# Four dense products of a hybrid encoder layer computed as seven block products of eight

## The chip, the cores and the metric

The kernel runs on one core of one Trainium2 chip. The metric is the device time of one execution in microseconds (us), the median of several runs. The profile is one further execution, recorded by the hardware profiler. PE is TensorE's matmul queue and PEld its weight loads, DVE is VectorE, ACT is ScalarE, POOL is GpSimd, SP the queue that issues the DMAs, SPq its issues.

## The reference, cut to what matters

512 positions and 16 meta positions of width 1024 pass one layer. Nothing but the products named here is changed:

```python
    y_conf = c @ w_conf_out                     # 1024 x 1024
    y_dn = o.reshape(b, l, HV) @ w_dn_out       # 1024 x 1024
    g_conf, g_dn = jnp.split(sigmoid(gate_logits + b_gate), 2, axis=-1)
    h = h + (g_conf * y_conf + g_dn * y_dn) @ w_out          # 1024 x 1024
    u2 = rmsnorm(h, norm_ffn_w)
    up = causal_dwconv(u2 @ w_up, ffn_dw_w, ffn_dw_b)        # 1024 x 5632, three taps
    f_gate, f_val = jnp.split(up, 2, axis=-1)
    return h + (jax.nn.silu(f_gate) * f_val) @ w_down
```

Before them stand one combined input projection, a causal convolution of 31 taps with a layer norm (it gives `c`), and a gated delta rule of 8 heads (it gives `o`). A final RMSNorm follows.

## The kernel before

Features lie on the 128 partitions and positions along the row, so an activation of width 1024 is eight tiles of 516 or 528 columns. Every dense product keeps float32 accuracy from operands split in two: `split` makes a rounded part `hi` (ScalarE) and the remainder `lo` (VectorE), and `gemm` sums `hi*hi`, `hi*lo` and `lo*hi` in one PSUM accumulation. For 128 output features that is 3 parts x 8 blocks of the depth x 2 halves of the positions, 48 matmuls of 258 or 260 columns, each with its own weight load. `weights` brings the 128 x 1024 weights of such a tile by a DMA on SP into `wr` (3 buffers), rounds them to `wh` on ScalarE and takes the remainder `wl` on VectorE (2 buffers each). The accumulators `p2` are two PSUM tiles of two banks each.

The order is: input norm and keys (`keys`), convolution gates (`glu`), the masked decays (`decays`, the only sizeable POOL work), Gram matrices (`grams`), `inverses` and `grow` (triangular inverses in 32-blocks), then the `heads` with gates `ga` and `z` between them. The 31 taps (`ca`) fill VectorE up to the end of the heads. Then come the delta-rule output projection (`gated`, tile `y`, operands `oh`, `ol`), the layer norm of the convolution and its output projection (`y` again, operands `ch`, `cl`), `w_out` (tile `wo`, operands `mh`, `ml`), the second norm and the feed-forward: `up` makes 44 output tiles, each scaled by the norm's `r` as it leaves PSUM (the norm is not needed before the product), and three taps make `uy` from it. Two `uy` give `fh` and `fl`, and `w_down` (tile `dn`) ends the layer.

Nothing runs in the order in which it is written. `Plan` records every instruction, `order` simulates five in-order engines with modelled costs (`price`), buffers (`SLOTS`) and priorities (`BIAS` and the named offsets), and `emit` issues the resulting fixed order through one helper line. So all instructions of the trace have the line of that helper, and they are told apart by tiles. What is fixed at build time is the order on each engine: where an instruction waits on the chip, all behind it on its engine wait too.

Of the kernel before, what the change touches and what calls it, by code (L numbers as in the profile page):

```python
# [19 lines left out]
P = 128  # L20
# [16 lines left out]
ROW = T + PAD  # L37

# [82 lines left out]
class Op:  # L121
    _fields = ("eng", "fn", "a", "k", "prio", "deps", "succ", "late", "wait", "cost", "ready", "end", "tiles", "lat", "table", "mode", "act", "tail", "alone")
# [21 lines left out]
TURN = {(False, True): 92, (True, False): 105, (True, True): 190}  # L144
# [6 lines left out]
STAY = 750  # L151
SWITCH = 600

BIAS = {'iv': -1500, 'd0': 100, 'v4': 40, 'v2': 100, 'z1': -570, 't11': -280, 't7': 350, 'k0': -70, 'ln': 250, 's7': -320, 'z0': -700, 'o2': 100, 'o5': 1600, 'd5': -650, 'g3': 150, 'd1': 2160, 'k2': -30, 'q7': -1720, 'k5': -30, 's4': -830, 'w3': -3100, 't2': -670, 'c5': -130, 't8': -40, 'o4': -350, 'q6': 350, 'g4': -350, 't4': -350, 'o1': 250, 'q4': -60, 't9': -750, 'z2': -600, 'o0': -600, 'g0': 30, 'q3': 500, 'q5': 100, 'c6': -30, 's1': -130, 't15': -100, 't1': -730, 's3': -470, 'y0': 250, 't12': -150, 'o6': 700, 'o3': -500, 'k4': -100, 'w2': 250, 't5': -150, 'v0': 30, 'g6': -120, 'z3': 250, 'g5': -190, 'q2': -70, 'y7': -30, 's5': -70, 'v6': -100, 'g1': -250, 'g7': 250, 'm4': 100, 'q0': -250, 'c7': -130, 'd3': -1750, 'o7': 100, 'm6': 30, 'm1': 30, 's6': -100, 'd2': -100, 'y6': 70, 'g2': -600, 'k6': -30, 'z4': -500, 't6': 100, 't3': 250}
LNP = 74
IVP = 1295
UP = 519
WP = 30
# [23 lines left out]

AFTER = 24
# [3 lines left out]
PARTS = (slice(1, 3), slice(0, 1))  # L187

# [9 lines left out]
class Plan:  # L198
# [9 lines left out]
    @contextmanager  # L208
    def at(self, by, late=True):
        if isinstance(by, str):  # L210
            by, late = BIAS.get(by, 0), False
        was = self.late
        self.prio, self.late = self.prio + by, was or late and by > 0
        yield
        self.prio, self.late = self.prio - by, was

    def add(self, eng, fn, a, k):
# [28 lines left out]
        if eng == "PE" and fn == "matmul":  # L246

            up = lambda n: 32 if n <= 32 else 64 if n <= 64 else P
            o.mode = (up(args[1].shape[0]), up(writes[0].shape[0]))
            o.mode = None if o.mode == (P, P) else o.mode  # L250
        o.cost, o.lat = self.price(eng, fn, a, k, writes[0])
        o.alone = self.price(eng, fn, a, k, writes[0], True)[0] if o.mode else o.cost
# [11 lines left out]
    def price(self, eng, fn, a, k, out, alone=False):  # L264
        n = out.n
        if eng == "PE":
            lhs, rhs = (k["lhsT"], k["rhs"]) if fn == "matmul" else (a[1], a[2])
            n = rhs.n
            if fn == "transpose":
                return 110, 0  # L270

            if out.ap.offset // out.tl.row and not alone:
                return 22, 0
# [3 lines left out]
            if lhs.shape[0] == 64:  # L277
                return 115, 0
# [13 lines left out]
    def order(self):  # L292
# [16 lines left out]
        table, dma, low, done = None, 0.0, 0, bytearray(len(ops))  # L309
        win, act, cold = 0, 0.0, True  # L310
        mode = None
# [14 lines left out]
        def look(e, t):  # L326

            q, nxt, best = ready[e], later[e][0][0] if later[e] else None, None
            for p, i in q:
# [26 lines left out]
                if e == "PE" and mode and o.mode != mode:  # L356
                    p += STAY
                elif o.table and table not in o.table:
                    p += SWITCH
# [4 lines left out]
        while len(out) < len(ops):  # L364
# [26 lines left out]
            if e == "PE":  # L391

                while t >= (win + 1) * WIN:
                    if act < LOW * WIN:
                        cold = True
                    elif act > HIGH * WIN:
                        cold = False
                    win, act = win + 1, 0.0
                if o.mode != mode:
                    c = o.alone + TURN[bool(mode), bool(o.mode)]  # L400
                if cold:
                    c *= 2
                act += o.act * (2 if cold else 1)
                mode = o.mode
            free[e] = t + c
            o.end = free[e]
            if e == "SP":
                dma = max(dma, t + 950) + o.lat
                o.end = dma + o.tail
            out.append(i)  # L410
# [10 lines left out]
            drain = 110 if o.mode else 0  # L421
            for j in o.succ:
                s = ops[j]
                s.ready = max(s.ready, o.end + LAT[e][s.eng] + (drain if s.eng != e else 0))
# [25 lines left out]
def record(A, out):  # L450
# [52 lines left out]
    def gemm(acc, ws, ah, al, ranges, k0=0, kn=None, first=True, last=True):  # L503
# [6 lines left out]
        for i, (k, w, a) in enumerate(runs):  # L510
            for b, (c0, c1, *at) in enumerate(ranges):
                p0 = at[0] if at else 0
                PE.matmul(acc[:, b, p0:p0 + c1 - c0], lhsT=w[:, k * P:(k + 1) * P], rhs=a[k0 + k][:, c0:c1],
                          start=first and i == 0, stop=last and i == len(runs) - 1)

# [263 lines left out]
    def decays(h):  # L779
# [5 lines left out]
                        compare_op=ALU.is_ge, fill=-1e30)  # L785
        for n in range(NC):
            S.activation(out=ev[:, n], in_=ev[:, n], func=AF.Exp, bias=ngc[:, n, h:h + 1])
# [46 lines left out]

    ivt = {}
# [136 lines left out]
    oh, ol = [], []  # L972
# [3 lines left out]
    def heads(h):  # L976
# [8 lines left out]
        with plan.at(f"s{h}"):  # L985
# [39 lines left out]
            for n in range(NC):  # L1025
# [18 lines left out]
                if n < NC - 1:  # L1044
                    s = s1

# [22 lines left out]
    def outs(h):  # L1069
# [5 lines left out]
        with plan.at(f"o{h}"):  # L1075
# [5 lines left out]
            a, b = split(z[:, :TW], TW, "o")  # L1081
            oh.append(a)
            ol.append(b)
# [38 lines left out]
    def gated(t, wsrc, ah, al):  # L1122
        acc = p2("y")
        gemm(acc, weights(wsrc), ah, al, MIDR)
        V.scalar_tensor_tensor(out=halves(t[:, :TW], HW), in0=halves(t[:, :TW], HW), scalar=1.0, in1=acc[:, :, MID],
                               op0=ALU.add, op1=ALU.mult)
        return t


    chh, chl = [], []  # L1130

    def layer_norm():
# [11 lines left out]
        for f in range(KT):  # L1144
            V.tensor_tensor(out=cacc[f][:, :TW], in0=cacc[f][:, :TW], in1=rl[:, :TW], op=ALU.mult)
            S.activation(out=cacc[f][:, :TW], in_=cacc[f][:, :TW], func=AF.Silu, scale=pc('lw', f), bias=pc('lb', f))
            a, b = split(cacc[f][:, :TW], TW, "c")
            chh.append(a)
            chl.append(b)
# [3 lines left out]
    ydn = [call(lambda f: gated(gts[KT + f], A['wdn'][f], oh, ol), "y", f) for f in range(KT)]  # L1153

    mh, ml = [], []
    for f in range(KT):
        y = call(lambda f: gated(gts[f], A['wco'][f], chh, chl), "c", f)
        V.tensor_tensor(out=y[:, :TW], in0=y[:, :TW], in1=ydn[f][:, :TW], op=ALU.add)
        a, b = split(y[:, :TW], TW, "m")
        mh.append(a)  # L1160
        ml.append(b)
# [4 lines left out]
    hs, hh, hl, sq = [], [], [], []  # L1166
    for f in range(KT):
        x = bt(n="xr")
        SY.dma_start(out=x[:, :TW], in_=A['xT'][f][:, T0:T])
        acc = p2("wo")  # L1170
        gemm(acc, weights(A['wo'][f]), mh, ml, MIDR)
        V.scalar_tensor_tensor(out=halves(x[:, :TW], HW), in0=acc[:, :, MID], scalar=0.5, in1=halves(x[:, :TW], HW),
                               op0=ALU.mult, op1=ALU.add)
        hs.append(x)
        hi, lo = bt(F32R, "hh"), bt(F32R, "hl")
        S.mul(out=hi[:, HS:HS + TW], in_=x[:, :TW], mul=pc('nf', f))
        V.scalar_tensor_tensor(out=lo[:, HS:HS + TW], in0=x[:, :TW], scalar=pc('nf', f), in1=hi.bitcast(F32)[:, HS:HS + TW],
                               op0=ALU.mult, op1=ALU.subtract)
        hh.append(hi)
        hl.append(lo)  # L1180
        s = bt(n="hsq")
        S.activation(out=s[:, :TW], in_=x[:, :TW], func=AF.Square)
        if f:
            V.tensor_tensor(out=s[:, :TW], in0=s[:, :TW], in1=sq[:, :TW], op=ALU.add)
        sq = s
    r2v = []
# [8 lines left out]
    def up(t):  # L1195
# [4 lines left out]
        u = bt(n="up")  # L1200
        uv = halves(u[:, :516], 258)
        for b in range(2):
            V.tensor_tensor(out=uv[:, b], in0=acc[:, b, :258], in1=r2v[b], op=ALU.mult)
# [9 lines left out]
    for t in range(FT):  # L1213
        g = up(t)
        S.activation(out=g[:, :SEQ], in_=g[:, :SEQ], func=AF.Silu)
        v = up(FT + t)
        V.tensor_tensor(out=g[:, :SEQ], in0=g[:, :SEQ], in1=v[:, :SEQ], op=ALU.mult)
        a, b = split(g[:, :SEQ], SEQ, "f")
        fh.append(a)
        fl.append(b)  # L1220
    cuts = ((0, 8), (8, 8), (16, 6))

# [5 lines left out]
    for f in range(KT - 1):  # L1228
# [3 lines left out]
        o = hs[f]  # L1232
# [9 lines left out]
    o, s = hs[f], bt(n="fsq")  # L1242
    for b in range(2):
# [14 lines left out]
        for i in range(0, KT, 2):  # L1258
            y = bt(n="fin")[:, :SEQ].rearrange("p (f t) -> p f t", f=2)
            for j in range(2):  # L1260
                V.tensor_tensor(out=y[:, j], in0=hs[i + j][:, ch], in1=rb[:, :hw], op=ALU.mult)
# [32 lines left out]

def _cols(v):
# [3 lines left out]
def arrays(x, meta_tokens, norm_mix_w, w_in, b_gate, conf_dw_w, conf_dw_b, conf_ln_w, conf_ln_b, w_conf_out,  # L1299
# [8 lines left out]
    a['wco'], a['wdn'], a['wo'] = _pack(w_conf_out[0]), _pack(w_dn_out[0]), _pack(w_out[0])  # L1308
    a['wup'], a['wd'] = _pack(w_up[0]), _pack(w_down[0])
# [29 lines left out]
```

## Time and profile before

| | us |
|---|---|
| median of 3 runs | 1037.63 (1037.09 to 1038.33) |
| the profiled execution | 1037.14 |
| its span, first to last instruction | 1035.4 |
| PE busy in it | 1019.7 |
| DVE busy | 717.1 |
| ACT busy | 476.7 |
| POOL busy | 8.4 |

The rows that the text rests on follow below. Busy times are sums over an engine; matmuls are pipelined, so that the pace of PE is read from how many matmuls lie in a piece of the chain and how long the piece is, not from the duration of one. For the other engines, too, an instruction's duration is a little longer than the distance to the next start.

### The profile page before, as it was taken

The numbers are of one execution on the slowest core, as the hardware profiler recorded it, in microseconds if no ns is written. First come the engines' busy times: TensorE is split into PE (matmuls) and PEld (weight loads), VectorE is DVE, ScalarE is ACT, GpSimd is POOL, SyncE is SP. The second block draws the span as 40 slices with busy tenths as digits, with TensorE's granted clock in tenths as the row PEclk, the third lists the DMA queues.
The fourth block names the chain that finished last, engine by engine and source line by source line (L and its number), as shares of the span: only waits on it lengthen the run. The fifth ranks groups of instructions, "written<-read, shape, count | busy, mean of one in ns | idle before, by whom it ended". The sixth has DMA issues, their size and how long they took to land.

```text
span 1035.4 us, 20014 instructions
## 1 busy us (share of the span) xinstructions
PE 1019.7 (98%) x8430; PEld 978.8 (95%) x8430; DVE 717.1 (69%) x1237; ACT 476.7 (46%) x847; POOL 8.4 (1%) x45
## 2 busy tenths in 40 slices
PE   9999999998999999999999999999999999999996
PEld 7999999998999999999999999999999999988886
DVE  5985699996599999996266555667676767623323
ACT  5787622446645565453254233544444444422222
POOL 0000000000000000000000000000000000000000
PEclk9999999997999999999999999999999999999998
DMA  6143333241121241214214332222222222333332
GB/s 220 63 135 93 100 108 111 83 123 52 43 97 54 67 132 54 93 62 144 82 42 153 115 121 82 86 100 83 101 86 99 82 103 84 95 92 92 97 92 82
DMA packets 44042, 98.40 MB, mean 95 GB/s; under 512 B 12720, under 2 KB 19248, under 8 KB 43952
## 3 DMA queue, kind: packets, MB, share of 16 engines
q1 hardware_dynamic: 43952, 97.12, 28.7%
q8 instruction: 66, 1.08, 0.4%
q14 instruction: 24, 0.20, 0.1%
HBM read 93.89 MB, written 3.21 MB: 94 GB/s over the span
## 4 chain that ended last, share of the span: by engine, by line
PE 92%; DVE 3%; ACT 3%; DMA 1%; issue 1%; SPq 0%; POOL 0%; DVEq 0%; ACTq 0%; POOLq 0%
PE up L447 25%; PE dn L447 12%; PE ga L447 9%; PE y L447 9%; PE z L447 5%; PE v L447 5%; PE wo L447 5%; PE q L447 4%; PE cv L447 4%; PE cg L447 3%; PE k L447 2%; PE o L447 2%; PE rs L447 1%; PE S L447 1%; PE wP L447 1%; DVE cv L447 1%
## 5 line engine op out<-in xcount | busy, mean ns | idle before, releaser
L447 DVE TENSOR_TENSOR wl<-wr,wh 128x1024 fp32r<-128x1024 f32 x157 | 189.3, 1206 | 156.7 <-PE dn L447 59.8
L447 ACT CAST wh<-wr 128x1024 fp32r<-128x1024 f32 x157 | 162.6, 1037 | 250.2 <-PE dn L447 57.5
L447 DVE SCALAR_TENSOR_TENSOR ca<-c,par,ca 128x516 f32<-128x516 f32 (+13 forms) x240 | 175.5, 742 | 3.1 <-ACT ca L447 0.3
L447 PE MATMUL up<-hh,wh 128*128 128x258 f32 x704 | 141.6, 282 | 0.0
L447 PE MATMUL up<-hl,wh 128*128 128x258 f32 x704 | 141.3, 282 | 0.0
L447 PEld LDWEIGHTS up<-hh,wh 128*128 128x128 f32 x704 | 109.2, 190 | 0.2 <-issue 0.2
L447 PEld LDWEIGHTS up<-hl,wh 128*128 128x128 f32 x704 | 108.7, 189 | 0.0
L447 PE MATMUL up<-hh,wl 128*128 128x258 f32 x704 | 91.9, 283 | 0.0
L447 PEld LDWEIGHTS up<-hh,wl 128*128 128x128 f32 x704 | 87.5, 190 | 0.0
L447 PE MATMUL dn<-fh,wh 128*128 128x512 f32 (+1 forms) x198 | 71.7, 370 | 0.0
L447 PE MATMUL dn<-fl,wh 128*128 128x512 f32 (+1 forms) x198 | 71.2, 368 | 0.0
L447 DVE SCALAR_TENSOR_TENSOR uy<-up,par,uy 128x512 f32<-128x512 f32 x88 | 65.9, 749 | 2.8 <-ACT uy L447 1.3
L447 DVE TENSOR_TENSOR up<-up,r 128x258 f32<-128x258 f32 x88 | 33.5, 420 | 47.1 <-PE up L447 44.3
L447 ACT ACTIVATE uy<-up,par 128x512 f32<-128x512 f32 x44 | 35.9, 816 | 55.4 <-DVE up L447 55.4
L447 PE MATMUL ga<-uh,wh 128*128 128x258 f32 (+1 forms) x256 | 56.9, 287 | 0.0
L447 PE MATMUL ga<-ul,wh 128*128 128x258 f32 (+1 forms) x256 | 56.6, 288 | 0.0
L447 DVE SCALAR_TENSOR_TENSOR cv<-ra,par,cv 128x528 f32<-128x528 f32 x69 | 51.3, 759 | 0.2
L447 PE MATMUL dn<-fh,wl 128*128 128x512 f32 (+1 forms) x198 | 45.4, 369 | 0.0
L447 PE MATMUL ga<-uh,wl 128*128 128x258 f32 (+1 forms) x256 | 44.6, 289 | 0.0
L447 PEld LDWEIGHTS dn<-fh,wh 128*128 128x128 f32 x198 | 37.2, 188 | 7.0
L447 PEld LDWEIGHTS dn<-fl,wh 128*128 128x128 f32 x198 | 37.2, 188 | 6.6
L447 PEld LDWEIGHTS ga<-uh,wh 128*128 128x128 f32 x256 | 42.1, 190 | 0.2
(284 smaller groups left out, 2195.9 us busy)
## 6 DMA issues: line engine op xcount, KB each, us to landing
wr<-in_win SPq DMA_DIRECT2D x64, 512.0 KB
wr<-in_wup SPq DMA_DIRECT2D x44, 512.0 KB
wr<-in_wd SPq DMA_DIRECT2D x17, 512.0 KB
wr<-in_wdn SPq DMA_DIRECT2D x8, 512.0 KB
wr<-in_wco SPq DMA_DIRECT2D x8, 512.0 KB
wr<-in_wo SPq DMA_DIRECT2D x8, 512.0 KB
wr<-in_wd SPq DMA_DIRECT2D x8, 384.0 KB
x<-in_xT SPq DMA_DIRECT2D x8, 264.0 KB
```

The lines of the kernel that those rows point to most:

```text
L447: getattr(engines[o.eng], o.fn)(*(get(x) for x in o.a), **{n: get(x) for n, x in o.k.items()})
```

## The change

Output tiles are taken in pairs (256 features). `_quarters` reorders the weights so that the four 512 x 128 quarters of a pair lie side by side, and `seven` forms the pair from seven products of 12 matmuls (3 parts x 4 blocks of the depth, 258 columns), 84 where two tiles took 96. Two PSUM banks `X` and `Z` serve all seven in turn; a product that is only an intermediate is added up in the bank after ScalarE or VectorE has read it (`use`). Three of the four activation operands and five of the weight operands are sums: `factors` makes the activation sums from two feature tiles on VectorE and splits them, and `presums` makes the weight sums in DRAM, by five DMAs issued by POOL for each pair, three of them with addition. 31 pairs are treated so: 4 of each output projection, 4 of `w_out`, 19 of `w_up`; 3 pairs of `w_up` (`NPRE`) stay as they were. The 19 take a normalised input (`xn`) made after the second norm. The residual `hs` is stored to DRAM (`d_h`) and loaded again (`back`) for the last stage. The model of the engines in `order` and its priorities are other ones, so that the whole order is computed anew.

```diff
@@ Plan.order (model of the engines)
-TURN = {(False, True): 92, (True, False): 105, (True, True): 190}
+PART, INTO, OUTOF = 0.833, 90, 95
-STAY = 750
+STAY = 1875
-LNP = 74
-IVP = 1295
-UP = 519
-WP = 30
+LNP = -1426
+IVP = 0
+UP = 2869
+WP = 74
+NPRE = 3
+            if eng == "POOL":
+                return 1000, int(np.prod(out.shape)) * 4 / 140.0
+                dma = max(dma, t + 1350) + o.lat * (1.5 if soft > t else 1)
+            elif o.fn == "dma_start":
+                soft = max(soft, t + 2000) + o.lat
+                o.end = soft + 1500
...
+    def presums(src, n, hold):
+        r = [plan.tile("dram", "con", [P, 4, HD], F32, "ws") for _ in range(n)]
+        for m in range(n):
+          with plan.at(1):
+            h = {hold} | ({softs[-2]} if len(softs) > 1 else set())
+            plan.after = set(h)
+            G.dma_start(out=r[m][:, 0:2], in_=src[:, m, 0:3:2])
+            plan.after = set(h)
+            G.dma_start(out=r[m][:, 2:4], in_=src[:, m, 0:2])
+            G.dma_start(out=r[m][:, 1:3], in_=src[:, m, 3:4].broadcast_to([P, 2, HD]), accum_op=ALU.add)
+            G.dma_start(out=r[m][:, 0], in_=r[m][:, 1], accum_op=ALU.add)
+            G.dma_start(out=r[m][:, 3], in_=r[m][:, 0], accum_op=ALU.add)
+            softs.append(len(plan.ops) - 1)
+        return r
+
+    def seven(src, m, sums, B, w, use):
+        acc = p2("se")
+        X, Z = acc[:, 0, :w], acc[:, 1, :w]
+        flat = lambda v: v.rearrange("p b c -> p (b c)")
+        tiles = (flat(src[:, m, 0:2]), flat(sums[m][:, 0:2]), flat(sums[m][:, 2:4]), src[:, m, 2])
+        for i, (b, to, first, what) in enumerate((('b11', X, True, 'p1'), ('b21', Z, True, 'c11b'),
+                                                  ('t2', X, False, 'u2'), ('t1', Z, True, 'c22b'),
+                                                  ('t3', X, False, 'u3'), ('b22', Z, False, 'c12b'),
+                                                  ('t4', X, False, 'c21'))):
+            if i % 2 == 0:
+                with plan.at("sw"):
+                    hi, lo = weights(tiles[i // 2], D if i < 6 else HD)
+            n, c = len(B), i % 2 * HD
+            runs = [(k, x, y) for part in PARTS for k in range(n) for x, y in ((lo, 0), (hi, 0), (hi, 1))[part]]
+            for j, (k, x, y) in enumerate(runs):
+                PE.matmul(to, lhsT=x[:, c + k * P:c + (k + 1) * P], rhs=B[k][b][y], start=first and j == 0, stop=j == len(runs) - 1,
+                          skip_group_check=not first)
+            use(what, to)
+
+    def quarters(src, m, sums, B, w, n):
+        c = [bt(n=n), bt(n=n)]
...
+            if what in ('p1', 'u2'):
+                S.copy(out=q(i, j), in_=acc)
+            elif what in ('c22b', 'c21'):
+                S.mul(out=q(i, j), in_=acc, mul=-1.0)
+            else:
+                V.tensor_tensor(out=q(i, j), in0=q(i, j), in1=acc, op=ALU.subtract if i else ALU.add)
...
+    def factors(x0, x1, w, n, hold=None):
...
+        V.tensor_tensor(out=TT[:, 0], in0=X0[:, 0], in1=X0[:, 1], op=ALU.subtract)
+        V.tensor_tensor(out=X0[:, 1], in0=X1[:, 1], in1=X0[:, 1], op=ALU.subtract)
+        V.scalar_tensor_tensor(out=TT[:, 1], in0=TT[:, 0], scalar=-1.0, in1=X1[:, 1], op0=ALU.mult, op1=ALU.subtract)
+        t4 = bt(n=n + "q")
+        V.scalar_tensor_tensor(out=t4[:, :w], in0=TT[:, 1], scalar=-1.0, in1=X1[:, 0], op0=ALU.mult, op1=ALU.subtract)
...
+            S.copy(out=sub(hi), in_=v)
+            V.tensor_tensor(out=sub(lo), in0=v, in1=sub(hi.bitcast(F32)), op=ALU.subtract)
...
+    wds, wcs, wos = (presums(A[n], KT // 2, masks[-1]) for n in ('wdn', 'wco', 'wo'))
+    wus = presums(A['wuq'], FT - NPRE, masks[-1])
...
-    def gated(t, wsrc, ah, al):
-        acc = p2("y")
-        gemm(acc, weights(wsrc), ah, al, MIDR)
-        V.scalar_tensor_tensor(out=halves(t[:, :TW], HW), in0=halves(t[:, :TW], HW), scalar=1.0, in1=acc[:, :, MID],
-                               op0=ALU.add, op1=ALU.mult)
+    def gated(m, wsrc, sums, B, ts):
+        for c, t in zip(quarters(wsrc, m, sums, B, HW, "yc"), ts):
+            V.scalar_tensor_tensor(out=t[:, :TW], in0=t[:, :TW], scalar=1.0, in1=c[:, :TW], op0=ALU.add, op1=ALU.mult)
...
+            ob.append(factors(zs[h - 1], zs[h], HW, "o", vals[-1]))
...
+            cb.append(factors(*cacc[f - 1:f + 1], HW, "c", dns[f // 2]))
...
+        mb.append(factors(*ys, HW, "m"))
...
+        for f in range(0, KT, 2):
+            with plan.at(f"h{f}"):
+                ab = []
+                for i in range(2):
+                    x = bt(n="xn")
+                    for b in range(2):
+                        V.scalar_tensor_tensor(out=x[:, b * 258:(b + 1) * 258], in0=hs[f + i][:, 2 + 256 * b:260 + 256 * b],
+                                               scalar=pc('nf', f + i), in1=r2v[b], op0=ALU.mult, op1=ALU.mult)
+                    ab.append(x)
+                ub.append(factors(*ab, 258, "n"))
...
+        if t < NPRE:
+            g, v = up(t), up(NPRE + t)
+        else:
+            g, v = quarters(A['wuq'], t - NPRE, wus, ub, 258, "up")
```

`hold` in `presums` is the last mask of `decays`; a chain of five also waits for the last DMA of the chain two before it (`softs[-2]`).

## Rows read from the trace of the kernel before

**Rows 1.** The page: busy time of each engine.
```profile
PE 1019.7 (98%) x8430; PEld 978.8 (95%) x8430; DVE 717.1 (69%) x1237; ACT 476.7 (46%) x847; POOL 8.4 (1%) x45
```
**Rows 2.** Chain that ended last: start, length, instructions (projections, `w_out`, feed-forward).
```profile
572.71 25.62 PE y L447 x211
598.34 46.67 PE wo L447 x384
...
654.64 0.90 PE rc L447 x8
655.53 244.45 PE up L447 x2037
899.99 114.76 PE dn L447 x528
```
**Rows 3.** Stages by stretches: busy time (instructions) of each engine, PEclk, DMA share, GB/s.
```profile
235.00:300.00 65.00, 61.05 (x795) 58.59 (x794) 41.63 (x68) 37.00 (x92) 0.58 (x5) 0.89 0.18 63
300.00:474.00 174.00, 174.00 (x1489) 168.49 (x1488) 166.23 (x257) 91.23 (x186) 0.87 (x10) 1.00 0.24 80
474.00:499.00 25.00, 25.00 (x210) 25.00 (x209) 14.10 (x17) 10.69 (x14) 0.00 (x0) 1.00 0.40 130
499.00:598.00 99.00, 98.98 (x914) 98.09 (x913) 53.55 (x70) 40.40 (x56) 0.00 (x0) 1.00 0.30 105
598.00:645.00 47.00, 47.00 (x389) 46.94 (x389) 24.97 (x31) 17.69 (x23) 0.00 (x0) 1.00 0.27 96
645.00:900.00 255.00, 255.00 (x2130) 254.63 (x2129) 173.39 (x262) 108.52 (x137) 0.00 (x0) 1.00 0.27 91
```
**Rows 4.** Instruction groups by form, all stretches: count, busy us, mean ns, idle before.
```profile
L447 DVE TENSOR_TENSOR wl<-wr,wh 128x1024 fp32r<-128x1024 f32 x149 | 181.7, 1219 | 141.5 <-PE dn L447 48.4 <-ACT wh L447 34.3 <-PE y L447 19.4
L447 ACT CAST wh<-wr 128x1024 fp32r<-128x1024 f32 x149 | 156.0, 1048 | 245.9 <-PE dn L447 53.3 <-PE up L447 45.6 <-PE y L447 30.6
L447 ACT COPY o<-o 128x128 f32<-128x128 f32 x32 | 8.5, 265 | 14.9 <-PE o L447 14.9
L447 ACT COPY ra<-q 128x528 f32<-128x528 f32 x8 | 4.8, 600 | 9.8 <-PE q L447 9.7
```
**Rows 5.** DVE in order of time, around 506, 523, 541 and 656 us: start, length.
```profile
505.19 1.23 DVE L447 TENSOR_TENSOR wl<-wr,wh 128x1024 fp32r<-128x1024 f32 x1 [4.57 <-PE y L447]
506.33 0.68 DVE L447 SCALAR_TENSOR_TENSOR gt<-gt,y 128x516 f32<-128x516 f32 x1
...
522.90 4.94 DVE L447 TENSOR_TENSOR ca<-ca,mean 128x516 f32<-128x516 f32 x8 [2.19 <-ACT mean L447]
...
655.98 0.76 DVE L447 TENSOR_TENSOR up<-up,r 128x258 f32<-128x258 f32 x2 [2.82 <-ACT r L447]
```
**Rows 6.** All engines in order of time, an `up` tile leaving PSUM and the taps.
```profile
700.55 1.53 DVE L447 SCALAR_TENSOR_TENSOR uy<-up,par,uy 128x512 f32<-128x512 f32 x2
...
702.06 2.09 PE L447 MATMUL up<-hh,wl 128*128 128x258 f32 x16
...
704.18 0.76 DVE L447 TENSOR_TENSOR up<-up,r 128x258 f32<-128x258 f32 x2 [2.10 <-PE up L447]
```
**Rows 7.** POOL in order of time: a mask, the last mask, memsets up to the last.
```profile
72.63 0.63 POOL L447 TENSOR_SCALAR_AFFINE_SELECT E<-E 128x512 f32<-128x512 f32 x1 [0.66 <-DMA E<-d_g]
...
115.41 0.63 POOL L447 TENSOR_SCALAR_AFFINE_SELECT E<-E 128x512 f32<-128x512 f32 x1 [14.74 <-DMA E<-d_g]
...
198.04 0.30 POOL L447 MEMSET LL<- 32x256 f32 x1 [81.92 <-ACT wh L447]
...
400.51 0.10 POOL L447 MEMSET ra<- 128x4 f32 x1 [12.79 <-PE S L447]
```
**Rows 8.** DVE in order of time, beside the mask at 72.63.
```profile
72.67 1.49 DVE L447 SCALAR_TENSOR_TENSOR Em<-Em,gc,cst 16x16 f32<-16x16 f32 x7 [2.04 <-DMA Em<-d_gm]
```
**Rows 9.** SP's issues in order of time: a store of 512 KB and the loads that need it.
```profile
217.08 0.38 SPq L447 DMA_DIRECT2D d_x<-XT  x1
...
222.42 3.51 SPq L447 DMA_DIRECT2D DU<-d_x  x4
```
**Rows 10.** Chain that ended last: a load of 256 KB, from issue to its reader.
```profile
107.72 7.57 DMA E<-d_g
115.41 0.63 POOL E L447
```
**Rows 11.** The page, DMA queues: packets, MB, share of 16 engines.
```profile
q1 hardware_dynamic: 43952, 97.12, 28.7%
```

More of the change, by code (lines that the diff above doesn't have):

```diff
@@ L121 @@
 class Op:
-    _fields = ("eng", "fn", "a", "k", "prio", "deps", "succ", "late", "wait", "cost", "ready", "end", "tiles", "lat", "table", "mode", "act", "tail", "alone")
+    _fields = ("eng", "fn", "a", "k", "prio", "deps", "succ", "late", "wait", "cost", "ready", "end", "tiles", "lat", "table", "mode", "act", "tail", "part", "size")
 class Rec:
@@ L187, with __init__, run @@
 PARTS = (slice(1, 3), slice(0, 1))
+class Array:
+    def __init__(self):
+        self.win, self.act, self.cold, self.mode, self.drain, self.tiles = 0, 0.0, True, None, 0.0, {}
+    def run(self, o, t):
+        while t >= (self.win + 1) * WIN:
+            if self.act < LOW * WIN:
+                self.cold = True
+            elif self.act > HIGH * WIN:
+                self.cold = False
+            self.win, self.act = self.win + 1, 0.0
+        x = 2 if self.cold else 1
+        self.act += o.act * x
+        if o.mode != self.mode:
+            t = max(t, self.drain) + (INTO * x if o.mode and not self.mode else 0)
+            self.mode, self.tiles = o.mode, {}
+        if not o.mode:
+            return t + o.cost * x, t + o.cost * x
+        t = max(t, self.tiles.get(o.part, 0.0))
+        n, m = o.size
+        self.tiles[o.part] = t + PART * (n + m) * x
+        end = t + (PART * n + OUTOF) * x
+        self.drain = max(self.drain, end)
+        return t + 7 * x, end
 def hit(a, b):
@@ L212, in at @@
         was = self.late
-        self.prio, self.late = self.prio + by, was or late and by > 0
+        self.prio, self.late = self.prio + by, was or late
         yield
@@ L391, in order @@
             if e == "PE":
[L393 to L406, printed above, removed]
+                free[e], o.end = array.run(o, t)
+            else:
+                free[e] = o.end = t + c
             if e == "SP":
-                dma = max(dma, t + 950) + o.lat
+                dma = max(dma, t + 1350) + o.lat * (1.5 if soft > t else 1)
                 o.end = dma + o.tail
+            elif o.fn == "dma_start":
+                soft = max(soft, t + 2000) + o.lat
+                o.end = soft + 1500
             out.append(i)
@@ L1146, in layer_norm @@
             S.activation(out=cacc[f][:, :TW], in_=cacc[f][:, :TW], func=AF.Silu, scale=pc('lw', f), bias=pc('lb', f))
-            a, b = split(cacc[f][:, :TW], TW, "c")
-            chh.append(a)
-            chl.append(b)
     with plan.at(LNP), plan.at("ln"):
         layer_norm()
[L1153 to L1161, printed above, removed]
+    ydn, dns = [], []
@@ L1188, in second_norm @@
+    d_h = [con([P, SEQ], "d_h", "dram") for _ in range(KT)]
+    for f in range(KT):
+        SY.dma_start(out=d_h[f], in_=hs[f][:, 4:TW])
+    r2v, ub = [], []
     def second_norm():
@@ L1212, in record, with ffn, ends, back @@
     fh, fl = [], []
-    for t in range(FT):
-        g = up(t)
+    def ffn(t):
+        if t < NPRE:
+            g, v = up(t), up(NPRE + t)
+        else:
+            g, v = quarters(A['wuq'], t - NPRE, wus, ub, 258, "up")
+        with plan.at("tp" if t < NPRE else "tq"):
+            ends(t, g, v)
+    def ends(t, g, v):
+        g = taps3(g, t)
         S.activation(out=g[:, :SEQ], in_=g[:, :SEQ], func=AF.Silu)
-        v = up(FT + t)
+        v = taps3(v, FT + t)
         V.tensor_tensor(out=g[:, :SEQ], in0=g[:, :SEQ], in1=v[:, :SEQ], op=ALU.mult)
-        a, b = split(g[:, :SEQ], SEQ, "f")
+        if t < FT - 3:
+            a, b = split(g[:, :SEQ], SEQ, "f")
+        else:
+            hl = plan.tile("sb", "iv", [P, D], F32R, "fv")
+            a, b = hl[:, :SEQ], hl[:, SEQ:]
+            S.copy(out=a, in_=g[:, :SEQ])
+            V.tensor_tensor(out=b, in0=g[:, :SEQ], in1=a.bitcast(F32), op=ALU.subtract)
         fh.append(a)
         fl.append(b)
+    for t in range(FT):
+        call(ffn, "u", t)
     cuts = ((0, 8), (8, 8), (16, 6))
+    hr = []
+    def back(f):
+        o = bt(n="hr")
+        SY.dma_start(out=o[:, 4:TW], in_=d_h[f])
+        hr.append(o)
+        return o
     def wdown(f, i):
@@ L1241, in record @@
     f, hw, ws = KT - 1, SEQ // 2, {}
-    o, s = hs[f], bt(n="fsq")
+    o, s = back(f), bt(n="fsq")
     for b in range(2):
```

139 lines of the change are left out of this document (95 added, 44 removed).

## The prediction

> **What bounds the kernel now.** I read the page's busy times first, then the chain that ended last, then the stages by stretches, and only then single instructions. PE is busy for 98% of the span [rows 1], and from the end of the heads the chain is PE alone: projections, `w_out`, feed-forward and `dn` follow each other without a gap [rows 2]. There time is matmuls times pace. 384 of `wo` took 46.67 us, 0.1215 each (half have 258 columns, half 260); 2037 of `up` took 244.45 us, 0.1200 each at 258 [rows 2]. The reader should see next, in the stretches, how much room the other engines have there: from 474 to 900 us DVE is busy 53 to 68% of each stretch, ACT at most 43%, DMA 27 to 40% [rows 3]. Before 474 it is otherwise: DVE 166 of 174 us from 300 to 474. So matmuls removed behind 474 are worth their full time as long as what replaces them fits into the room of DVE, and that room is what I add up.
>
> **What is removed.** 31 pairs of tiles at 12 matmuls. The three small products lose 144 of 1152, and the 1008 that stay are all 258 columns wide: 1152 x 0.1215 - 1008 x 0.1200 = 140.0 - 121.0 = 19.0 us. `up` loses 19 x 12 = 228: 27.4 us. Together **-46.4 us**, which is all that PE can give.
>
> **What DVE gets.** Prices go by the distance to the next start. `wl` 1.14 us (505.19 to 506.33); a 516-column instruction with two tensors 0.61 ((4.94 - 0.69) / 7); one of 258 columns 0.34 (0.76 for two, the second 0.42 long) [rows 5]. A pair needs 3.5 weight tiles where it needed 2, so 1.5 x 1.14 = 1.7 us more. `factors` has five instructions of 258 columns and three of 516, 5 x 0.34 + 3 x 0.61 = 3.5 us, where two splits took 1.2: 2.3 more. Leaving PSUM, DVE reads three products of 258 columns in a projection's pair (1.0 us), on top of the gates that it already multiplies; seven in a `wo` pair where it read two of 516 (2.4 for 1.2); three in an `up` pair where it read four (-0.3). By stretch, with the busy times of [rows 3]:
> From 474 to 499: 14.1 + 4 x 2.3 (operands of the delta rule, held until its last value) = 23.3 of 25 us.
> Projections: 53.6 + 8 x (1.7 + 1.0) + 8 x 2.3 (operands of the convolution, and of `wo`) = 93.6 us, where PE needs 672 x 0.12 = 80.6 and some 5 for the layer norm's sums and their spreading, 86. **DVE is 8 us over.**
> `wo`: 25.0 + 4 x (1.7 + 1.2) = 36.6 of 40.3.
> Feed-forward: 173.4 + 19 x (1.7 - 0.3) + 16 x 0.34 (`xn`) + 4 x 3.5 = 219.4 of 1884 x 0.12 + 1.3 = 227.4 us.
> So over this whole part DVE goes from 266.0 of 426 us to 373 of 379: PE and DVE are level. ACT gets 46.5 more casts of 1.05, some 108 evictions of 0.37 (between 0.265 at 128 columns and 0.600 at 528 [rows 4]) and the factors' copies, about 110 us on 177: it keeps a quarter of its time. The residual's stores and loads (16 DMAs of 256 KB) stand beside a DMA share under 0.3 and cost nothing while their waits come late; without that cover one is the 7.57 us of a dependent load [rows 10].
>
> **Where it stands in the way.** Five places, each with both ends.
> (1) The 8 us of DVE too many in the projections. `wo`, the next stage, has 4 of room and 474 to 499 has 2, so between 0 (the last split and gates slide) and 8; I take 4, half, as the room is half the excess.
> (2) Projections to `wo`. Every first product needs all four pairs of `m` factors. After the last product come eviction, two gates, two adds, the sums, a copy and a split: 0.4 + 2 x 0.67 + 2 x 0.61 + 4 x 0.34 + 0.6 + 0.6, 5.5 us before the first operand of the last pair is complete; two `seven`s begun on three blocks of four cover 2 x 2 x 9 x 0.12 = 4.3. Ends 0 and 8 (no cover, and the rest of the factors), taken 3, since the other operands follow on DVE.
> (3) Second norm. `r` is there at 655.5, 10.5 us into the stage [rows 2]; the six tiles kept last 6 x 48 x 0.12 = 34.6, which leaves 24 us. In it DVE has 12 evictions (4.1), five weight tiles (5.7), `xn` (5.4) and four factors (14.0): 29.2. Ends 0 (the 4.3 us of started blocks hide it) and 9 (the taps of a tile come between); taken 4.
> (4) The banks. A product lasts 12 x 0.12 = 1.44 us, and five of the seven reuse the bank of the product but one before. An eviction of `up` began 0.31 us after its last matmul's start (702.06 + 15 x 0.12 = 703.87, then 704.18) and takes 0.42 [rows 6]; with as much again for the way back the turn is about 1.0, so 0.4 us are free. A `wl` or a tap in front on DVE (1.14, 0.75) breaks that. Ends per pair: 0, and 5 x 0.7 = 3.5 us. The fixed order can put the eviction first and PE can take the second accumulator's products, so I stay near the low end, 0.2 us a pair: 6 us for 31.
> (5) POOL. Its DMAs stand in order with four `LL` memsets and the `ra` memsets of the heads, which came between 198 and 400 us [rows 7]; a DMA that waits for an earlier one holds these, then the ScalarE copy that fills `ra`, the head's convolution and PE behind. A wait is 5.3 us (a store to its reader's issue [rows 9]) to 7.6 [rows 10]. Ends 0 and two such waits, 15; taken 2. The new order may also win: PE's clock was 0.89 of full from 235 to 300, where PE was idle for 4 us [rows 3], 7 us at most; I take nothing for it.
> Sum: 1037.1 (the profiled time; it is 0.5 under the median) - 46.4 + 4 + 3 + 4 + 6 + 2 = 1009.7, with 0.5 for the median **1010 us**.
>
> **Rivals.** *All of it arrives.* The stalls hide as the fixed order is made for them; for it speaks that no PE idle at all is left behind 300 now, against it the 8 us of DVE in (1). 1037.6 - 46.4 = 991 us; with 3 from a better early part 988. Chance 0.15.
> *DVE sets the pace.* It is level with PE in sum, and a queue in order that waits for ACT and PE never fills: from 300 to 474 it was busy 166.2 of 174, 96% [rows 3]. At 93%, 373 us become 401 where PE alone needs 379, and with (2), (3) and (5) the time is 991 + 22 + 9 = 1022, at 90% 1035. Chance 0.15.
> *Slower: the banks.* If PE waits at every reuse, 155 waits cost more than the change saves from 46.4 / 155 = 0.30 us each. At 0.4 it is 991 + 62 = 1053 us. For it speaks that DVE will be busy 96% of the feed-forward, with 1.14 us pieces against 0.4 of room; against it the second accumulator and ACT, which takes four of the seven in two stages. Chance 0.11.
> *The sums come late.* POOL's chains start after the last mask at 115.4 [rows 7], two in flight. Each has four dependent links of 5.3 to 7.6 us [rows 9, 10], so one ends every 11 to 15 us and the last of 31 at 450 to 590, while the first of `up`'s is needed at about 640. The 65 MB that they write are, at the 97.12 MB in 28.7% of the span [rows 11], 199 us of DMA. If one chain took 25 us instead, the last would come at 891, its pair 12 later and `dn` to the end 135 more: 1038, no gain left; at 28 us, 116 + 868 + 12 + 135 = 1131 us. Chance 0.05. A mask beside a VectorE instruction with two SBUF inputs took the same 0.63 us as one without [rows 7, 8], so I see no hold of POOL by VectorE.
> The Trainium skill, page "SBUF — State Buffer", section "SBUF: two separate sides", gives this rival its mechanism: descriptors of a DMA issued from GpSimd are made by GpSimd, and it is locked out of the shared port while VectorE runs in a two-port mode. By the page's section "Who interferes with whom" tensor_tensor has no such mode, and tensor_tensor and its like are nearly all that VectorE runs here, so by that rule the chains keep the pace of the links; no DMA of POOL is in this trace to show it.
>
> **How the numbers follow.** My forecast has 0.54, its own range 996 to 1022 (all terms at a third or at twice their size, roughly). A measurement tells 0.2%, 2 us. Faster holds the forecast, the first rival, and most of the second (0.14): 0.83. Slower holds 0.10 of the banks and 0.03 of late sums: 0.13. The rest, 0.04, lies within 0.2%. For the range I leave out the slower cases and the lowest part of the first rival: 988 to 1035.
>
> **What would show it.** Right: `wo` with 336 matmuls and `up` with 1884 at 0.120; DVE about 373 us busy where PE needs 379; PE gaps of some us in front of `wo` and of the first `seven` of the feed-forward, and a few tenths at bank reuses; POOL's last DMA before 640. Wrong: gaps in front of most products named after DVE or ACT evictions; PE waiting for `wh` or `wl` with a DMA behind them; heads later than 474 behind a POOL memset; a granted clock under 1.00 behind 474. What I can't see is the new fixed order, and it decides (4) and (5).

## The result, and the profile after

The change made the kernel slower: 1154.12 us, median of four runs (1153.39 to 1170.26), against 1037.36 (1037.02 to 1038.33) for the kernel before in the same session; ratio 1.1168, 95% interval 1.1084 to 1.1252. The forecast was 1010 us with a range up to 1035, so both the time and the sign were wrong. The profiled execution below is the longest of the four, 1170.26 us with a span of 1168.5; stage lengths are read from it, and differences between kernels from medians.

The page's busy times (they answer to [rows 1]) and its DMA queues ([rows 11]):

```profile
PE 1039.2 (89%) x8058; PEld 958.3 (82%) x8058; DVE 831.3 (71%) x1444; ACT 583.1 (50%) x1059; POOL 136.9 (12%) x200
...
q1 hardware_dynamic: 55184, 125.70, 33.3%
q0 software_dynamic: 26288, 65.02, 28.8%
```

The work is what the forecast counted. PE has 8430 - 8058 = 372 matmuls fewer, 144 + 228. DVE has 114 us more (forecast 107), ACT 106 more (forecast 110). But PE, 98% busy before, stands still for 129 us of the span. The stretches show where ([rows 3] is the same view of before; columns as there):

```profile
522.00:579.00 57.00, 46.59 (x331) 42.35 (x332) 37.27 (x61) 25.56 (x43) 13.20 (x17) 0.97 1.00 233
579.00:638.00 59.00, 47.49 (x329) 42.78 (x328) 36.05 (x56) 23.66 (x40) 11.48 (x13) 0.94 0.88 240
638.00:718.00 80.00, 58.71 (x343) 52.35 (x344) 45.62 (x77) 27.31 (x39) 6.62 (x8) 0.81 0.65 183
...
757.00:1033.00 276.00, 221.06 (x1595) 197.79 (x1594) 188.20 (x263) 150.96 (x232) 0.00 (x0) 1.00 0.42 131
```

The heads end at 522 us (499 before). From top to bottom: the two projections take 57 and 59 us for 336 matmuls each, which at 0.12 us are 40.3; `w_out` with its handover takes 80; and behind the three pairs of `up` in the old way (39 us, left out here) the 19 feed-forward pairs take 276 us, 14.5 a pair where 84 x 0.12 = 10.1. In that last stretch DVE and ACT are far from full, DMA is at 0.42 and the granted clock at 1.00. So none of these sets the pace there. The waits of this stretch (who waited for what: us in total, times, longest) name it:

```profile
DVE up L469 <- PE se L469: 60.0, 54, 1.5
...
PEld se L469 <- DVE up L469: 37.6, 51, 0.8
PEld se L469 <- ACT up L469: 37.4, 55, 1.2
...
PE se L469 <- DVE up L469: 27.3, 51, 0.6
PE se L469 <- ACT up L469: 25.8, 54, 1.0
```

PE waits for evictions 105 times in 19 pairs, and the evictions wait for PE. A stop holds PE's weight loads for 0.7 us (75.0 us in 106 waits). These are the gaps "named after DVE or ACT evictions" that the prediction gave as a sign that it is wrong. The chain that ended last, a piece of a pair in the steady state ([rows 2] had one piece of 2037 matmuls here):

```profile
903.32 0.38 ACT up L469
903.70 0.04 issue
903.74 1.86 PE se L469 x13
...
905.65 0.04 issue
905.69 0.44 DVE up L469
906.13 0.04 issue
906.17 1.24 PE se L469 x8
907.41 0.02 issue
907.43 0.38 ACT up L469
```

PE and an eviction take turns; nothing overlaps. What an eviction waits for is seen instruction by instruction (all engines in order of time: start, length, engine, operation, and the idle time before it):

```profile
904.22 0.65 PE L469 MATMUL se<-nh,wl 128*128 128x258 f32 x4
...
904.70 0.28 PE L469 MATMUL se<-nh,wh 128*128 128x258 f32 x1
...
905.31 0.28 PE L469 MATMUL se<-nl,wh 128*128 128x258 f32 x1
...
905.69 0.42 DVE L469 TENSOR_TENSOR up<-up,se 128x258 f32<-128x258 f32 x1 [1.23 <-PE se L469]
...
906.17 0.39 PE L469 MATMUL se<-nh,wh 128*128 128x258 f32 x1 [0.59 <-DVE up L469]
```

A product ends with four matmuls on `wl`, here those at 904.22. At 904.70 the next product begins, in the other bank, and issues six matmuls. DVE has been idle since 904.46, yet it reads the finished product only at 905.69, right after the sixth matmul of the *other* bank; and the seventh matmul into that other bank starts only after DVE's read has ended. So each side waits for the other although they touch different banks. The changed program's list of instructions says the same: the waits on evictions stand in the middle of products.

```
5514 L469 MATMUL se_30_11119<-nh_7_8706,wh_187_11093 128x258
5515 L469 MATMUL se_30_11119<-nl_7_8725,wh_187_11093 128x258 [waits Activation_49]
5516 L469 MATMUL se_30_11119<-nh_10_8777,wh_187_11093 128x258
```

`X` and `Z` are two slices of one PSUM tile (`acc = p2("se")`), and the waits are set for the tile: an eviction of `X` waits for whatever matmul into `Z` stands before it in the order, and the next matmul into `Z` waits for that eviction. The stops, up to six a pair, make 75.0 / 19 = 3.9 of the 4.4 us by which 14.5 exceeds 10.1. That was my theory after this reading; the rivals were the traffic of the sums (DMA share 0.65 to 1.00 up to 718 us) and the long handovers. In all kernels of the experiments ties between buffers are broken by a counter, where the kernels before and after the change compare addresses; what else is changed is shown.

### The profile page after: what moved, and what is told of

It reads as the page before. It is cut to its first block, busy times and chain, and to the rows that moved or that the text cites. A ratio compares the mean times of both kernels' runs of the same rounds, so it can differ in the third digit from the quotient of the medians.

```text
span 1168.5 us, 20291 instructions
## 1 busy us (share of the span) xinstructions
PE 1039.2 (89%) x8058; PEld 958.3 (82%) x8058; DVE 831.3 (71%) x1444; ACT 583.1 (50%) x1059; POOL 136.9 (12%) x200
## 3 DMA queue, kind: packets, MB, share of 16 engines
q1 hardware_dynamic: 55184, 125.70, 33.3%
q0 software_dynamic: 26288, 65.02, 28.8%
## 4 chain that ended last, share of the span: by engine, by line
PE 66%; DVE 19%; DMA 7%; ACT 5%; issue 3%; SPq 0%; DVEq 0%; ACTq 0%
PE se L469 28%; PE dn L469 11%; PE ga L469 6%; PE z L469 4%; DVE wl L469 3%; DVE ca L469 3%; PE q L469 3%; PE v L469 3%; DMA wr<-ws 2%; DVE up L469 2%; DMA orb<-d_r 2%; ACT up L469 2%; PE k L469 2%; PE o L469 1%; DVE cv L469 1%
## 5 line engine op out<-in xcount | busy, mean ns | idle before, releaser
L469 ACT CAST wh<-wr 128x1024 fp32r<-128x1024 f32 (+2 forms) x219 | 214.1, 978 | 318.3 <-PE se L469 108.5
L469 DVE TENSOR_TENSOR wl<-wr,wh 128x1024 fp32r<-128x1024 f32 (+2 forms) x219 | 248.4, 1136 | 129.7 <-PE dn L469 60.8
L469 DVE SCALAR_TENSOR_TENSOR ca<-c,par,ca 128x516 f32<-128x516 f32 (+11 forms) x240 | 177.0, 746 | 2.9
L469 PE MATMUL se<-nh,wh 128*128 128x258 f32 x456 | 122.0, 295 | 27.0 <-ACT up L469 17.2
L469 PE MATMUL se<-nl,wh 128*128 128x258 f32 x456 | 120.2, 290 | 16.1 <-DVE up L469 8.5
L469 PEld LDWEIGHTS se<-nh,wh 128*128 128x128 f32 x456 | 85.4, 189 | 37.8 <-ACT up L469 24.5
L469 PEld LDWEIGHTS se<-nl,wh 128*128 128x128 f32 x456 | 85.4, 189 | 23.1 <-DVE up L469 12.0
L469 POOL DMA_DIRECT2D ws<-ws x62 | 58.5, 944 | 166.0 <-DMA ws<-ws 72.6
L469 PE MATMUL se<-nh,wl 128*128 128x258 f32 x456 | 75.1, 284 | 3.1 <-DVE up L469 1.6
L469 PEld LDWEIGHTS se<-nh,wl 128*128 128x128 f32 x456 | 63.1, 190 | 4.5 <-DVE up L469 2.3
```

The costliest lines, as they stand in the source:

```text
L469: getattr(engines[o.eng], o.fn)(*(get(x) for x in o.a), **{n: get(x) for n, x in o.k.items()})
```

## The experiments

**One PSUM tile or two, sums or none.** Four combinations, the changed kernel being the one with a shared tile and with sums. `e1` gives `Z` a tile of its own:

```diff
-        X, Z = acc[:, 0, :w], acc[:, 1, :w]
+        X, Z = acc[:, 0, :w], p1("sz")[:, :w]
```

`Z` then comes from the pool of one-bank tiles, which has four in turn, so that successive pairs have more banks as well; within a pair, where the stops lie, `Z` has one bank in both. `e2` makes no sums (no DMA on POOL) and loads as much raw weight instead, so that it multiplies other weights than the reference, as `e3`, `e6` and `e7` do:

```diff
-        tiles = (flat(src[:, m, 0:2]), flat(sums[m][:, 0:2]), flat(sums[m][:, 2:4]), src[:, m, 2])
+        tiles = (flat(src[:, m, 0:2]), flat(src[:, m, 0:2]), flat(src[:, m, 2:4]), src[:, m, 2])
-    wds, wcs, wos = (presums(A[n], KT // 2, masks[-1]) for n in ('wdn', 'wco', 'wo'))
-    wus = presums(A['wuq'], FT - NPRE, masks[-1])
+    wds = wcs = wos = wus = None
```

`e3` does both.

> The second accumulator Z of a block product gets a PSUM tile of its own; everything else as in the changed kernel, the order planned anew. Theory of the shared tile (an eviction waits for the matmuls issued before it into either bank of the tile, and the next matmul into either bank waits for the eviction; six such stops of 0.7 us in each of 31 pairs): the 19 pairs of the feed-forward go from 14.5 us each to about 10.3, 80 us less, and the projections and w_out lose some 25 more where DMA doesn't hold them: about 1045 us, from 1153. Rival, waits for the same bank that come from a full VectorE and ScalarE: the pace of the pairs stays at 13 to 14.5 us, and the time over 1120. Rival, late sums and DMA: no change behind 757 us of the trace, over 1140.

> The DMAs that add up the weights in DRAM are left out, and raw quarters of the weights are loaded in place of the sums, as many bytes by as many loads; so the products are of the wrong weights. One PSUM tile as in the changed kernel. Theory of DMA (the sums' traffic slows SP's loads and stores from 116 to 700 us): the start of the first projection comes back from 522 to about 499 us, the waits for the summed weights (9, 8 and 10 us) go, and the time falls by about 50 to 1100 us; the pace in the feed-forward stays at 14.5 us a pair, which is the shared tile's. If the sums cost nothing but those three waits: about 1125. If they were the whole loss: about 1010.

> Both at once: a tile for each accumulator, and no sums in DRAM (wrong weights in three of four loads). If the two causes are all, the time is that of the prediction's sum without its DMA, 991 to 1010 us, and pairs take 10.1 to 10.5 us in every stage. If a third cause is left (the operands' sums on VectorE, the handover to w_out and to the feed-forward), it is over 1025 us and shows as gaps of PE at those handovers.

| median us (ratio to before, interval) | shared tile | two tiles |
|---|---|---|
| with sums | 1154.12 (the change) | 1061.33 (1.0237, 1.0195 to 1.0278) |
| without sums | 1151.07 (1.1096, 1.1067 to 1.1126) | 1026.05 (0.9899, 0.9883 to 0.9916) |

The shared tile costs 92.8 us with the sums and 125.0 without them. The sums cost 3.1 us under a shared tile and 35.3 once the tile waits are gone: the two causes cover each other, and whoever removes only the sums sees almost nothing (the 3.1 us lie within the spread of the changed kernel's runs, 1153.39 to 1170.26). 92.8 and 3.1 hold the other way of breaking ties too, 125.0 and 35.3 do not. `e1` was expected at about 1045 us and `e2` at about 1100; neither expectation had the sums cost so little under the shared tile and so much without it. Of 1154 - 1010 = 144 us missed, 92.8 are the tile, 35.3 the sums, 16 something else; as the forecast held 6 us for the banks and 2 for POOL, it was 24 short elsewhere. A piece of the chain of `e1` in the feed-forward:

```profile
798.32 1.43 PE se L470 x12
799.75 1.45 PE sz L470 x12
801.19 1.44 PE se L470 x12
802.63 1.45 PE sz L470 x12
804.07 2.90 PE se L470 x24
```

Product follows product at 1.44 us; the chain is PE alone here, and the 19 pairs take 201.2 us (726.4 to 927.6), 10.6 each. The reads now lie beside matmuls (`e1`, all engines in order of time):

```profile
799.78 0.37 ACT L470 COPY up<-se 128x258 f32<-128x258 f32 x1 [0.33 <-PE se L470]
799.83 0.28 PE L470 MATMUL sz<-nh,wh 128*128 128x258 f32 x1
```

The accumulators were in two banks before this edit and after it; only the tile differs. The Trainium skill, page "PSUM — Partial Sum Buffer", section "PSUM bank collisions raise a hardware error", asks that PSUM be guarded by bank, so by that rule the wait across two banks is one that the program set and the chip did not ask for; the two rows agree, ScalarE reading `se` while TensorE writes `sz`.

**The feed-forward alone.** `e4` is the kernel before, with its own model and priorities (prices for POOL's DMAs, and for SP's beside them, are added), and with only the 19 pairs of `up` by seven products in two tiles; `e8` puts both accumulators back into one tile, `e7` makes no sums.

```diff
# e4, against the kernel before
+    wus = presums(A['wuq'], FT - NPRE, masks[-1])
...
+        if t < NPRE:
+            g, v = up(t), up(NPRE + t)
+        else:
+            g, v = quarters(A['wuq'], t - NPRE, wus, ub, 258, "up")
# e8, against e4
-        X, Z = acc[:, 0, :w], p1("sz")[:, :w]
+        X, Z = acc[:, 0, :w], acc[:, 1, :w]
```

> The kernel before, with its own costs and priorities up to the second norm, in which only the 19 pairs of the feed-forward are made of seven products, each accumulator in a PSUM tile of its own; 19 chains of sums from the last mask on, two in flight. Theory (stages before the feed-forward lost more to the sums' traffic, to doubled operand work on VectorE and to the handover than their 19 us of matmuls): pairs at 10.5 us where two tiles took 11.6, less some 4 us at the second norm, and some 5 of traffic beside the heads: 1037 - 20 + 4 + 5 = about 1026, faster by 1%. Rival (VectorE or the weight buffers set the pace of the feed-forward whatever stands before it, and traffic costs the heads over 15 us): 1037 or more.

> The kernel before with only the feed-forward's 19 pairs in seven products, with their sums, and both accumulators in one PSUM tile, as in the changed kernel. Theory (every eviction stops PE when both accumulators are one tile): a pair takes 14.5 us in place of 10.6, 19 x 3.9 = 74 us more than the 1030.65 of two tiles, about 1105 us, and nothing else moves. Rival (the stops of the changed kernel came from its model and its fixed order): this order has the costs of before, and a pair stays under 12 us, the whole under 1060.

> The kernel before with only the feed-forward's 19 pairs in seven products, two PSUM tiles, and no weight sums made (raw quarters of the weights are loaded in their place, so the feed-forward's weights are not those of the reference). With the sums the first projection began at 513 us, 14 later than before, and the whole took 1030.65 us. Theory (the traffic of the sums costs this): the first projection begins at 499 to 503 us and the whole takes 1013 to 1019 us. Rival (it is the newly computed order, with the sums hidden): the first projection still begins near 513 us and the whole stays within 3 us of 1030.65.

`e4` took 1030.65 us (0.9945, 0.9926 to 0.9964), `e8` 1114.97 (1.0737, 1.0683 to 1.0792), `e7` 1017.05 (0.9824, 0.9799 to 0.9848). In an order made with the costs of before, the shared tile still costs 84 us. By the profiles 78 of them lie in the 19 pairs, 4.1 each (280.3 us in place of 201.9; 74 were expected), and 4.5 ahead of the first projection (517.9 in place of 513.4). So the rival that the new model's order made the stops falls. The sums cost 13.6 us here, and `e7` begins its first projection at 498.7 us like the kernel before, while `e4` begins it at 513.4. So the sums cost 14 us ahead of the projections. The order of `e7` is planned without them and differs too; that it is their traffic is read from the chain. `e4`:

```profile
228.56 8.18 DMA d_x<-XT
...
239.64 11.68 DMA DU<-d_x
...
384.71 10.33 DMA orb<-d_r
```

and `e7`, whose longest pieces from 150 to 480 us hold one DMA:

```profile
365.69 6.43 DMA orb<-d_r
```

These are short dependent transfers of SP, a store and the load that needs it. [rows 9] had 5.3 us from that store's issue to its first load's issue; here the store alone takes 8.2 and its loads 11.7 more. Beside the sums such links take half as long again and more, and the heads hang on them. POOL's queue, by which term (5) had the heads held, did not do it: in the list of waits of `e4` no engine waits for a memset, and for POOL at all only ScalarE, twice, 3.3 us together, for masks.

**Which sums cost, and where.** `e6` is `e1` with the sums of the 12 early pairs only (raw weights in the feed-forward). `e5` is `e4` with one chain in flight instead of two. `e9` is `e4` with the chains held until the last value of the delta rule.

```diff
# e6, against e1
-    wus = presums(A['wuq'], FT - NPRE, masks[-1])
+    wus = None
# e5, against e4
-            h = {hold} | ({softs[-2]} if len(softs) > 1 else set())
+            h = {hold} | ({softs[-1]} if softs else set())
# e9, against e4 (the call now stands behind the heads)
-    wus = presums(A['wuq'], FT - NPRE, masks[-1])
+    wus = presums(A['wuq'], FT - NPRE, vals[-1])
```

> The changed kernel with a tile for each accumulator, in which only the 12 early pairs have their sums made in DRAM; the 19 pairs of the feed-forward load raw quarters in place of sums (wrong weights there). The sums then end at about 310 us. Against the version with all sums (1061 us) and the one with none (1026): if the loss of 35 us is traffic at the time of the projections and w_out, from sums that only the feed-forward needs, it is about 1035, and the first projection to the end of w_out takes 140 us as without sums. If it is that the early sums are late or their loads slow by themselves, it stays at 1050 to 1061.

> The same with one chain of sums in flight instead of two, 19 chains of some 20 us from 116 us on. If it is the share of the DMA engines that slows the heads, this is faster than two in flight, by 2 to 5 us. If what costs is GpSimd's queue, in which the heads' memsets stand behind waiting DMAs, it is the same or slower. If chains get late, the feed-forward waits for loads of summed weights, which would show behind 700 us.

> The same kernel with two tiles, its 19 chains of sums held until the last value of the delta rule (near 474 us) in place of the last mask (115). Two in flight took 18 us a chain, 19 x 18 = 344 us, so the last comes near 820 where the last pair begins near 885. Theory (the sums cost in the crowded stretches up to the heads' end, and little behind): the first projection begins at 499 to 503 us and the whole takes 1015 to 1023 us. Rival (traffic costs the same wherever it stands): what is won ahead of the projections is lost in them and the whole stays at 1028 to 1033. If a chain takes 22 us or more, the last pairs wait for it and the whole is above 1035.

`e6`: 1039.89 us (1.0024, 1.0011 to 1.0037). So of the 35.3 us, 21 go with the feed-forward's sums, which run through the projections, and 14 are left with the early ones alone, which run through the heads. From the first projection to the end of `w_out` the profiles have 175 us in `e1` (from 513.3), 143 in `e6` (from 518.1) and 142 in `e3` (from 507.6). By place, then, `e1` loses 33 us in these stages and 6 ahead of them. The heads of `e6` end 5 us later than those of `e1`, though fewer sums run beside them; from 235 to 300 us the granted clock is 0.76 in `e6` and 0.89 in `e1`, so a part of the 14 us may be the order of `e6` and its clock and not the traffic. In `e1`, from 516 to 688 us, ACT waits 21.8 us for `wr` from `ws`; its stretches show DMA full and the clock under 1.00:

```profile
568.00:622.00 54.00, 43.35 (x330) 41.59 (x329) 36.45 (x59) 23.05 (x40) 13.25 (x17) 0.94 0.97 251
622.00:689.00 67.00, 49.24 (x352) 47.19 (x351) 44.72 (x75) 27.56 (x40) 9.85 (x11) 0.87 0.94 256
```

`e5`: 1028.65 us (0.9914, 0.9889 to 0.9939), which can't be told from `e4`. Its 19 chains take 27.2 us each (105 to 623 us) where two in flight gave one every 18.1; it spreads the same traffic thinner and wins nothing that is sure.

`e9`: 1049.06 us (1.0110, 1.0089 to 1.0132), slower than `e4`, and the theory that the sums cost little behind the heads fell. The chains began at 403.4 us and not near 474, and the first projection, expected at 499 to 503 us, begins at 508.0: the chain there holds a load of 9.59 us:

```profile
423.44 9.59 DMA eg<-d_e
```

The larger part is in the stretches of `e9`:

```profile
508.00:607.00 99.00, 98.97 (x913) 98.01 (x912) 53.58 (x70) 40.52 (x56) 22.40 (x27) 1.00 0.90 219
607.00:654.00 47.00, 47.00 (x389) 46.93 (x388) 24.98 (x31) 17.70 (x23) 10.66 (x13) 1.00 0.97 243
...
688.00:820.00 132.00, 114.02 (x839) 107.89 (x838) 104.19 (x150) 79.28 (x126) 12.54 (x16) 0.95 0.67 188
```

The old projections and `w_out` are not touched by a DMA share of 0.90 to 0.97: 99 and 47 us, to the microsecond those of [rows 3]. The seven-product pairs are: PE is busy 114.0 of their first 132 us, where in `e7`, without sums, it is busy 128.3 (678.6 to 810.6). An old tile of 48 matmuls lasts 5.8 us and needs one weight load; a pair needs 3.5 loads in 10.1 us, one every 2.9. That this is the difference is argued; no run tried it alone. The chain of `e9` there has pieces such as

```profile
691.91 9.78 DMA wr<-ws
...
712.35 9.11 DMA wr<-in_wuq
```

The last DMA of the chains was issued at 751 us, yet the pairs stay slow until some 820 (11.3 us each instead of 10.1). From 765 to 820 us DMA is waited for only 0.7 us. ScalarE waits 12.0 us for PE before it can write `wh`, and PE four times, 0.5 us each, for `wl`: this reads as a delay that the two buffers of each hand on from pair to pair, after the traffic that began it. No run tried more buffers.

**What is left without tile waits and sums.** `e3` stands 35 us over the 991 at which all of the saving would arrive. Its stretches have two places to show:

```profile
593.00:607.00 14.00, 6.74 (x35) 5.78 (x35) 13.17 (x25) 6.01 (x11) 0.00 (x0) 0.65 0.62 193
...
685.00:709.00 24.00, 21.63 (x177) 21.22 (x176) 24.00 (x39) 15.44 (x25) 0.00 (x0) 1.00 0.49 154
...
726.00:889.00 163.00, 163.00 (x1354) 162.66 (x1353) 147.29 (x210) 121.05 (x194) 0.00 (x0) 1.00 0.61 186
```

The first is the handover from the convolution's projection to `w_out`: DVE works 13.2 of 14 us, PE 6.7, and the granted clock is 0.65, that is, part of the stretch at the lower of its two levels, 1.2 GHz. The chain there, with PE idle for most of it:

```profile
597.00 1.14 DVE wl L470
598.13 0.61 DVE gt L470
598.74 0.61 DVE wl L470
...
599.40 1.24 PE se L470 x4
...
600.72 1.23 DVE wl L470
601.95 0.62 DVE gt L470
...
603.32 0.63 ACT mh L470
```

`wl` pieces for products that can't start yet stand in DVE's queue between the gates that the operands need. From 593.9 to 650.0 us `w_out` takes 56.1, 16 more than its 40.3 of matmuls. The second place is the start of the seven-product pairs, behind the second norm: DVE is busy for 24 us without a gap, and PE is not. From 726 us on PE is full and a pair takes 10.1 us, so that all that the feed-forward loses stands ahead of that: from 650.0 to 889.2 it takes 239.2 us where 1884 x 0.12 = 226.1, 13 more; before the change it was 255.0 for 2112 x 0.12 = 253.4, 1.6 more.

## Why the prediction was wrong, point by point

**The saving: right.** 372 matmuls, 46.4 us by the pace; where nothing holds PE, as in `e1` above, 12 matmuls take 1.44 us.

**The banks, term (4): the step that failed.** It said that "five of the seven reuse the bank of the product but one before", left 0.4 us of room at each, and took "0.2 us a pair: 6 us for 31". The room was worked out per bank, and the diff shows that both banks are one tile. The turn that I priced at about 1.0 us is nearly right as the price of a stop (0.7), but it is paid six times a pair with no product in between to hide it: 92.8 us in place of 6. The rival "Slower: the banks" had the right kind of sign and a break-even that was passed, but the same wrong cause, a reuse of the same bank; at 1053 us it was 101 too low, and 0.11 too small a chance. Asking of each `acc[:, 1]` which tile the waits are kept on would have given 31 x 6 x 0.7 = 130 us, and with it the sign.

**POOL and the sums, term (5) and the fourth rival: wrong in kind.** I priced the chains for being late and for holding POOL's memsets. They ended later than the 450 to 590 us that I had, at 676 us in the changed kernel, but not too late: the feed-forward's first seven-product pair began at 757. That 65 MB were "199 us of DMA" stood in the text, without a cost: by the page of after they are 28.8% of 1168 us, 336 us of all 16 engines, and in that time the DMA share is 0.65 to 1.00 in place of 0.18 to 0.40. Measured with two tiles: 35.3 us in place of 2. The pace of the links, 11 to 15 us a chain, came out at 18, with 8.4 us to landing for 512 KB and 6.3 for 256 KB (medians on the page). In `e5`, with one chain in flight, the medians are 7.3 and 5.2 us, and 7.3 + 7.3 + 5.2 + 5.2 = 25.0 us for a chain's four links are most of its 27.2. So no hold of POOL by VectorE is needed to explain that pace, which is what followed from the Trainium skill, page "SBUF — State Buffer", section "Who interferes with whom"; no run here tried the hold itself.

**The handovers, terms (2) and (3).** Both were mis-sized. At the second norm `e3` loses 13.1 - 1.6 = 11.5 us in place of 4, above the upper end of 9; all of it lies ahead of 726 us, where DVE is full for 24 us. The handover to `w_out` takes 16 us in place of 3. The 5.5 us of work that I counted are there, but `wl` pieces stand between them, and the clock fell during the gap, for which I had no term.

**DVE, term (1) and the second rival.** The load was right, and apart from those 24 us and the handover to `w_out`, DVE set the pace of no stretch behind the heads: `e3` runs the first two projections, layer norm included, in 86.3 us (507.6 to 593.9), where I counted 86 and 4 more.

**No term at all:** 9 us ahead of the projections. `e3` begins them at 507.6 us and `e7`, also without sums, at 498.7; the difference is the full change's own order and its extra work at the heads' end, and I did not take it apart. With the two handovers this makes 9 + 16 + 11.5 = 36.5 us, some 2 more than the 35 by which `e3` stands over 991; the other stages are that much shorter.

**What would beat both.** With two tiles, seven products in the feed-forward alone are faster than the kernel before, by 0.5% in `e4` and 0.9% in `e5`. The three small products by the same scheme, sums left out, gave nothing: `e3` is 9 us slower than `e7`. Weight sums that cost no traffic would be worth some 14 us more (`e7`), but as long as they are made on the chip that has to be paid for.

## What to carry to other kernels

Two accumulators overlap only if the waits are kept apart for them: before pricing a ping-pong between banks, see whether the two are one tile in the program, and price one stop for each eviction if they are. A background transfer that is never late is still not free; price it by what it does to the short dependent loads and to stages that load weights often, and look at where the DMA share already stands. And where two causes cover each other, take away both before judging either: the sums looked free (3 us) until the tile waits were gone (35 us).

## What the runs showed of the hardware that I had not expected

Copies and additions from DRAM to DRAM, issued by POOL, are dear: 65.02 MB took 28.8% of the 16 DMA engines' span where SP's 125.70 MB took 33.3%, so a megabyte costs 1.7 times as much, and 256 KB take 6.3 us to landing. A DMA share of 0.97 left a stage with one weight load in 5.8 us untouched (`e9`, 47.0 us for `w_out`). One with a load every 2.9 us, begun beside the end of the same traffic (share 0.67 from 688 to 820 us), had PE busy for 114.0 of 132 us where 128.3 were busy without it.
